# Seeding the banks of a down projection with the residual rows, in a decoder layer on one core

## The chip, the cores and the metric

The kernel is one program on 1 core of one Trainium2 chip. It computes one layer of a hybrid decoder on 256 rows of 2048 numbers, all in float32. The metric is device time in microseconds (us): the median of the runs.

The engines are named as in the profile: PE (TensorE, the products), PEld (its weight loads), DVE (VectorE), ACT (ScalarE), POOL (GpSimd) and SP, which issues most DMAs. A bank is one of the eight accumulators of 128 x 512 float32 in PSUM, into which PE writes its products and from which DVE and ACT read them.

## What is computed

The layer has three sub-layers, each followed by a LayerNorm over the sum of the scaled input and the sub-layer's result. The change is in the first and the third, two feed-forward networks (FFNs) of the same shape:

```python
D_MODEL, SEQ, D_FF = 2048, 256, 5632
DEEPNORM_ALPHA = (2.0 * DEPTH) ** 0.25        # DEPTH = 1
FFN_RES_WEIGHT = 0.5

def swiglu(x, w_gate, w_up, w_down):
    return (jax.nn.silu(x @ w_gate) * (x @ w_up)) @ w_down

x = layer_norm(DEEPNORM_ALPHA * x + FFN_RES_WEIGHT * swiglu(x, ffn1_w_gate, ffn1_w_up, ffn1_w_down), ln1_g, ln1_b)
# attention: two groups of heads, then layer_norm(DEEPNORM_ALPHA * x + mix, ln2_g, ln2_b)
x = layer_norm(DEEPNORM_ALPHA * x + FFN_RES_WEIGHT * swiglu(x, ffn2_w_gate, ffn2_w_up, ffn2_w_down), ln3_g, ln3_b)
```

A LayerNorm does not notice a common factor, so the kernel builds 2 * ALPHA * x + swiglu(x) and scales the epsilon by four.

## The kernel before

**Rows and products.** The 256 rows are two tiles t of 128. The residual stream lies in `y[t]`, 128 x 2048 in SBUF, in four column chunks n of 512. Every float32 product is made as three products of split numbers (`mm3`, lines 94 to 98): each operand is a high half (`whi` of a weight, `thi` of a row block) and a low half (`wlo`, `tlo`), and high x high (L96), high x low (L97) and low x high (L98) are added up in one bank. The halves are made by `split`: ACT casts the high half (L91), DVE subtracts it from the number to get the low half (L92).

**The blocks.** The work of an FFN is a list of steps (line 543): gate(0), up(0), gate(2), up(2), gate(4), down(0), up(4), gate(6), up(6), gate(8), down(1), up(8), then `last()` (the eleventh chunk of gate and up) and down(2). Gate and up make two chunks of 512 hidden columns each. After an up block the hidden columns are transposed by PE (`trans`, L463: four 128 x 128 transposes into one bank), copied out and split by ACT (L468, L470) and DVE (L471), while the next block runs. A down step takes the hidden columns of a group as the inner dimension and makes the four column chunks of the output: down(0) and down(1) have 8 pairs of inner blocks, down(2) has 6.

**One block (`gemm2`, line 251).** It makes a pair of column chunks j for both row tiles t, so four banks (t, j). The inner dimension comes in pairs i. A plain pair takes 8 `mm3`. A pair that is listed in `seven` takes 7, by Strassen's scheme: sums of the weights are made on DVE (L318 to L320) and sums of the rows (L390 to L393), and four of the products go to banks of their own, p1, p5, p6 and p7. Behind the last such pair these are read out once into four scratch tiles `rest` (L357 on ACT, L358 to L361 on DVE), while the plain pairs behind go on in the four banks (t, j). At the end of the block DVE adds each bank to its scratch tile (L370), and the block's `finish` is called with the result. So a block uses eight banks, and the pool has eight.

**What `finish` does.** For a gate block it is ACT's silu in place on the scratch tile (L479; in `last()` L510). For a down block it is `fin` (line 523), which adds the result to the rows: in down(0) `y = 2 * ALPHA * y + r` (L526), in down(1) and down(2) `y = r + y` (L528), each on DVE over 128 x 512. A down step calls `gemm2` twice, for the column pairs cp = 0 and 1; the second half of down(2) is made by `gemm` (line 540), chunk by chunk with 8 `mm3` a pair, and `fin` then reads the banks directly.

**What sets the order.** PE and SP keep the order in which the kernel's code issues their instructions. The instructions of ACT, DVE and POOL are put in an order by the scheduler, with its own costs, when the program is built; on the chip each engine works its queue off strictly in that order. A bank taken by `new_bank()` is free again when the last reader of its earlier tile is done. A block's pairs are in the order `DOWN` (4, 0, 1, 5, 2, 3, 6, 7), with 0 to 3 as the sevens; the first pair is plain, so it touches all four banks (t, j), in the order (0,0), (1,0), (0,1), (1,1), three products each.

Of the kernel before, what the change touches and what calls it, by code (L numbers as in the profile page):

```python
# [13 lines left out]
AF = mybir.ActivationFunctionType  # L14
OP = mybir.AluOpType
# [3 lines left out]
P = 128  # L19
D = 2048  # L20
S = 256
NT = S // P
FF = 5632
KD = D // P
NCH = 512
ALPHA = 2.0 ** 0.25
# [23 lines left out]
def layer(ctx: ExitStack, tc: tile.TileContext, a: dict, out: bass.AP):  # L50
    nc = tc.nc
    PE, V, A, G = nc.tensor, nc.vector, nc.scalar, nc.gpsimd
# [38 lines left out]
        A.copy(hi, src)  # L91
        V.tensor_tensor(lo, src, f(hi), op=OP.subtract)  # L92

    def mm3(ps, x, wh, wl, first, last):
        xh, xl = x
        PE.matmul(ps, xh, wh, start=first, stop=False)  # L96
        PE.matmul(ps, xh, wl, start=False, stop=False)  # L97
        PE.matmul(ps, xl, wh, start=False, stop=last)  # L98


    lanes, now, flags, held = {}, [0], {}, [False]
# [78 lines left out]
    def new_bank():  # L180
        return bank.tile([P, NCH], F32, name="bank")
# [66 lines left out]
                ahead[id(nxt[0]), nxt[1], nxt[2]] = load(nxt[0], nxt[1], [nxt[2] + j for j in range(KT)])  # L248
            finish(i, ps)

    def gemm2(x, xs, kps, seven, w, cp, finish, each=None, head=0, pre=None):

# [6 lines left out]
        B, todo = {}, []  # L261
# [10 lines left out]
        first, last = {}, {}  # L272
        for i, ops in todo:
            for o, op in enumerate(ops):
                first.setdefault(op[0], (i, o))
                last[op[0]] = (i, o)
        rest, heads = {}, []

        def weights(at, i):

# [45 lines left out]
        def mul(i, o, b, xp, name, wt):  # L326
            if b not in B:
                B[b] = new_bank()
            xp = sl(xs[i], xp) if isinstance(xp, int) else x(*xp)
            mm3(B[b], xp, *wt[name], first[b] == (i, o), last[b] == (i, o))  # L330

        for at, (i, ops) in enumerate(todo):
            if not s_at or at > s_at[-1]:
                held[0] = False
            wt = weights(at, i)
# [19 lines left out]
            if s_at and at == s_at[-1]:  # L355
# [6 lines left out]
                rest = {(0, 0): p1, (0, 1): q, (1, 0): u, (1, 1): z}  # L362
# [4 lines left out]
                each(at)  # L367
        for b in [(t, j) for t in range(NT) for j in range(2)]:
            if rest:
                V.tensor_tensor(rest[b], B[b], rest[b], op=OP.add)  # L370
            finish(*b, rest.get(b, B[b]))

    def new_T():
# [2 lines left out]
    def sl(pair, j):  # L376
        return pair[0][:, j, :], pair[1][:, j, :]


    ident = const.tile([P, P], F32, name="ident")  # L380
    make_identity(nc, ident)

    y = [const.tile([P, D], F32, name=f"y{t}") for t in range(NT)]
# [12 lines left out]
    def parts(s):  # L396
        hl = am2(F32R)
        split(*hl, s)
        return hl
# [48 lines left out]
    def ffn(name, x, xs, done, begin=None, after=None, late=()):  # L448
        wg, wu, wd = (W[name + n] + (W2[name + n][0],) for n in ("_w_gate", "_w_up", "_w_down"))
        groups = [[0, 1, 2, 3], [4, 5, 6, 7], [8, 9, 10]]  # L450
        late = list(late)
        hT, hS, hs, sg = {}, {}, {}, {}

        def trans(cs, ready, want=()):

            for c in cs:
                v, sums_too = [], c in want
                for t in range(NT):
                    while held[0] or now[0] < ready:
                        yield 1  # L460
                    pt = new_bank().rearrange("p (a b) -> p a b", a=4)
                    for j in range(4):
                        PE.transpose(pt[:, j, :], hs[c, t][:, j * P:(j + 1) * P], ident)  # L463
                    hT[c, t] = new_T()
                    src = pt
                    if sums_too:
                        src = wk([P, 4, P])
                        A.copy(src, pt)  # L468
                        v.append(src)
                    A.copy(hT[c, t][0], pt)  # L470
                    V.tensor_tensor(hT[c, t][1], src, f(hT[c, t][0]), op=OP.subtract)  # L471
                    if t and sums_too:
                        for i in range(KT):
                            hS[2 * c + i] = parts(sums([u[:, KT * i + j] for u in v for j in range(KT)]))
                    yield 1

        def gate(c0):
            def fin(t, j, r):
                A.activation(r, r, AF.Silu)  # L479
                sg[c0 + j, t] = r  # L480

            if c0:
                gemm2(x, xs, GATE, GATE7, name + "_w_gate", c0 // 2, fin)
                return
            def first(t, j, ps):
                sg[j, t] = wk([P, NCH])
                A.activation(sg[j, t], ps, AF.Silu)

            def rest(at):
                if begin and at == 7:  # L490
                    cst.update(load_consts())
                for _ in range(2):
                    if late:
                        late.pop(0)()

            gemm2(x, xs, GATE, (), name + "_w_gate", 0, first, each=rest, head=0 if begin else 4, pre=begin)

        def up(c0):
            def fin(t, j, r):
                hs[c0 + j, t] = sg[c0 + j, t]  # L500
                V.tensor_tensor(hs[c0 + j, t], r, sg[c0 + j, t], op=OP.mult)

            gemm2(x, xs, LATE if c0 in (4, 8) else UP, UP7, name + "_w_up", c0 // 2, fin, each=after if c0 == 0 else None)
            spawn(trans((c0, c0 + 1), now[0] + DFF, (0, 1, 4, 5, 9)), "T")

        def last():

            def fin(t, j, r):
                if j == 0:
                    A.activation(r, r, AF.Silu)  # L510
                    hs[10, t] = r
                else:
                    V.tensor_tensor(hs[10, t], r, hs[10, t], op=OP.mult)

            gemm2(x, xs, GATE, GATE7, name + "_gu", 0, fin)
            spawn(trans((10,), now[0] + DLAST), "T")

        def down(gi):
            grp = groups[gi]
            ks = list(range(grp[0] * 4, (grp[-1] + 1) * 4))  # L520
            xh = lambda k, t: sl(hT[k // 4, t], k % 4)

            def fin(t, n, ps):
                yc = y[t][:, n * NCH:(n + 1) * NCH]
                if gi == 0:
                    V.scalar_tensor_tensor(yc, yc, 2 * ALPHA, ps, op0=OP.mult, op1=OP.add)  # L526
                else:
                    V.tensor_tensor(yc, ps, yc, op=OP.add)  # L528
                if gi == 2:
                    done(t, n)  # L530

            for cp in range(2):
                if gi < 2 or cp == 0:
                    base = 2 * grp[0]
                    order, sevens = (DOWN, DOWN7) if gi < 2 else (range(6), (2, 3))
                    gemm2(xh, hS, [base + i for i in order], [base + i for i in sevens], name + "_w_down", cp,
                          lambda t, j, r: fin(t, 2 * cp + j, r))
                    continue
                for n in (2 * cp, 2 * cp + 1):
                    gemm(xh, wd, n, ks, lambda t, ps: fin(t, n, ps), tail=6 if n == 3 else 0)  # L540


        for step, n in ((gate, 0), (up, 0), (gate, 2), (up, 2), (gate, 4), (down, 0), (up, 4), (gate, 6), (up, 6), (gate, 8),
                        (down, 1), (up, 8)):
            step(n)
        last()
        down(2)
# [640 lines left out]
```

## Time and profile before

| | |
|---|---|
| median of 3 runs | 1764.81 us (1761.37 to 1767.2) |
| span of the profiled execution, first to last instruction | 1761.7 us |
| PE, PEld busy | 1741.7, 1429.6 us |
| DVE busy | 1596.9 us (2123 instructions) |
| ACT busy | 993.9 us (1306 instructions) |
| mean granted clock of TensorE | 0.998 |

The time of the profiled execution is known by its span; the median of the runs is 3.1 us above it. A row of the groups by line reads: line, engine, operation, result <- operands, shape, xcount | busy us, mean ns of one | idle time of the engine ahead of it, and what ended most of it. A row of a timeline reads: start in us from the span's start, how long, engine, line, operation, tiles, count, and in brackets the idle time ahead of it and what ended it; a row with x2 or x3 holds instructions that follow each other, with the time from the first's start to the last's end. A row of the list of waits reads: who <- whom, total us, times, longest us. A row of the windows reads: length, then for PE, PEld, DVE, ACT and POOL the busy us and the instructions, then PE's granted clock, the DMAs' share and their GB/s.

The first FFN runs from the start to about 697 us, the second from about 1060 us to the end. In the first, down(0) begins at 220, down(1) at 472 and down(2) at 638 us.

### The profile page before, as it was taken

Reading aid. Unit: us, or ns where it says so; the run is one execution under the profiler, and the core shown is the slowest. Engines: PE = TensorE matmul, PEld = TensorE weight load, DVE = VectorE, ACT = ScalarE, POOL = GpSimd, SP = SyncE. Lnnn points to the kernel's source line nnn. Section 1 sums busy time; section 2 is a strip of 40 time slices with the busy share of each in tenths; the row PEclk is TensorE's granted clock in tenths of the full one; section 3 lists DMA queues with packets and bytes.
Section 4 is the critical chain, followed back from the end, with each engine's and each line's share of the span. In section 5 each row is a group of like instructions: output and inputs, shape, how many; then the busy total and the mean of one; then the engine's idle time right before and its main releaser. Section 6 shows DMA issues by size and latency. Waiting matters only on the chain.

```text
span 1761.7 us, 22427 instructions
## 1 busy us (share of the span) xinstructions
PE 1741.7 (99%) x8058; PEld 1429.6 (81%) x8058; DVE 1596.9 (91%) x2123; ACT 993.9 (56%) x1306; POOL 17.0 (1%) x39
## 2 busy tenths in 40 slices
PE   9999999999999999999999999999999999999997
PEld 7888888888888888887788778888888878878886
DVE  7899999999999998765587679999999999999997
ACT  6656555574655565654455556565655565655651
POOL 0000000000000000000000000000000000000000
PEclk9999999999999999999999999999999999999999
DMA  9665666556656657545853355655566556556654
GB/s 334 218 211 178 204 204 203 191 184 212 197 196 225 204 172 255 181 139 206 283 195 111 132 168 179 203 179 203 192 206 222 201 181 215 191 193 217 203 200 159
DMA packets 103408, 350.01 MB, mean 199 GB/s; under 512 B 11136, under 2 KB 13696, under 8 KB 103296
## 3 DMA queue, kind: packets, MB, share of 16 engines
q1 hardware_dynamic: 102016, 344.39, 58.3%
q0 software_dynamic: 1280, 4.20, 0.9%
q8 instruction: 63, 1.03, 0.2%
q14 instruction: 49, 0.40, 0.1%
HBM read 346.44 MB, written 2.10 MB: 198 GB/s over the span
## 4 chain that ended last, share of the span: by engine, by line
PE 78%; DVE 14%; issue 3%; DMA 3%; ACT 2%; SPq 0%; DVEq 0%; POOL 0%; ACTq 0%; POOLq 0%
PE bank L97 24%; PE bank L96 24%; PE bank L98 24%; DVE wlo L92 6%; DVE sum L318 2%; DMA raw<-in_ffn_w_down 1%; DVE w L370 1%; ACT whi L91 1%; DVE sum L320 1%; DVE sum L319 1%; DMA raw<-in_ffn_w_up 1%; PE bank L1022 1%; DVE tlo L471 1%; PE bank L463 1%; PE bank L948 1%
## 5 line engine op out<-in xcount | busy, mean ns | idle before, releaser
L96 PE MATMUL bank<-whi,thi 128*128 128x512 f32 (+1 forms) x1934 | 761.6, 394 | 1.2 <-ACT whi L91 1.2
L97 PE MATMUL bank<-wlo,thi 128*128 128x512 f32 (+1 forms) x1934 | 751.6, 389 | 2.7 <-DVE wlo L92 2.5
L98 PE MATMUL bank<-whi,tlo 128*128 128x512 f32 (+1 forms) x1934 | 751.4, 389 | 0.0
L91 ACT CAST whi<-raw 128x1024 fp32r<-128x1024 f32 (+2 forms) x569 | 533.6, 965 | 272.1 <-PE bank L98 142.0
L92 DVE TENSOR_TENSOR wlo<-raw,whi 128x1024 fp32r<-128x1024 f32 (+2 forms) x569 | 624.8, 1113 | 53.5 <-ACT whi L91 52.6
L91 ACT CAST whi<-sum 128x1024 fp32r<-128x1024 f32 x267 | 278.9, 1050 | 366.4 <-DVE sum L320 140.1
L96 PEld LDWEIGHTS bank<-whi,thi 128*128 128x128 f32 x1934 | 363.2, 188 | 79.3 <-issue 4.1
L97 PEld LDWEIGHTS bank<-wlo,thi 128*128 128x128 f32 x1934 | 363.4, 188 | 75.9 <-DVE wlo L92 4.9
L98 PEld LDWEIGHTS bank<-whi,tlo 128*128 128x128 f32 x1934 | 363.0, 188 | 75.7
L92 DVE TENSOR_TENSOR wlo<-sum,whi 128x1024 fp32r<-128x1024 f32 x267 | 319.6, 1216 | 24.8 <-ACT whi L91 23.2
L97 PE MATMUL bank<-wlo,m 128*128 128x512 f32 x424 | 166.2, 392 | 2.4 <-DVE wlo L92 2.4
L98 PE MATMUL bank<-whi,m 128*128 128x512 f32 x424 | 165.1, 389 | 0.0
L96 PE MATMUL bank<-whi,m 128*128 128x512 f32 x424 | 165.0, 389 | 0.0
L318 DVE TENSOR_TENSOR sum<-raw 128x1024 f32<-128x1024 f32 x106 | 129.3, 1219 | 9.9 <-DMA raw<-in_ffn_w_down 5.4
L97 PEld LDWEIGHTS bank<-wlo,m 128*128 128x128 f32 x424 | 79.6, 188 | 22.6 <-DVE wlo L92 6.1
L96 PEld LDWEIGHTS bank<-whi,m 128*128 128x128 f32 x424 | 79.6, 188 | 16.8
L98 PEld LDWEIGHTS bank<-whi,m 128*128 128x128 f32 x424 | 79.6, 188 | 16.1
L370 DVE TENSOR_TENSOR w<-bank,w 128x512 f32<-128x512 f32 x120 | 79.0, 683 | 0.3
L320 DVE TENSOR_TENSOR sum<-sum,raw 128x512 f32<-128x512 f32 x106 | 72.6, 685 | 0.2
L319 DVE TENSOR_TENSOR sum<-sum,raw 128x512 f32<-128x512 f32 x106 | 72.6, 685 | 0.0
L773 ACT ACTIVATE w<-w,mx 128x256 f32<-128x256 f32 (+1 forms) x48 | 21.4, 446 | 30.4 <-DVE mx L769 27.4
L463 PEld LDWEIGHTS bank<-ident,w 128*128 128x128 f32 x176 | 21.9, 140 | 5.8
(188 smaller groups left out, 944.9 us busy)
## 6 DMA issues: line engine op xcount, KB each, us to landing
raw<-in_ffn_w_down SPq DMA_DIRECT2D x169, 512.0 KB, 4.8
raw<-in_ffn_w_up SPq DMA_DIRECT2D x160, 512.0 KB, 4.7
raw<-in_ffn_w_gate SPq DMA_DIRECT2D x146, 512.0 KB, 4.8
raw<-in_ffn_gu SPq DMA_DIRECT2D x32, 512.0 KB, 4.4
raw<-in_w_in SPq DMA_DIRECT2D x30, 512.0 KB, 4.8
raw<-in_w_out SPq DMA_DIRECT2D x20, 512.0 KB, 3.3
sum<-in_w_in SPq DMA_DIRECT2D x18, 512.0 KB, 5.9
sum<-in_ffn_w_gate SPq DMA_DIRECT2D x12, 512.0 KB, 4.4
```

Source lines behind the costliest of these rows:

```text
L91: A.copy(hi, src)
L92: V.tensor_tensor(lo, src, f(hi), op=OP.subtract)
L96: PE.matmul(ps, xh, wh, start=first, stop=False)
L97: PE.matmul(ps, xh, wl, start=False, stop=False)
L98: PE.matmul(ps, xl, wh, start=False, stop=last)
L318: V.tensor_tensor(t13, a_, b_[:, 1:2, :].broadcast_to([P, 2, NCH]), op=OP.add)
L319: V.tensor_tensor(t24[:, 0], t13[:, 0], a_[:, 1], op=OP.add)
L320: V.tensor_tensor(t24[:, 1], t24[:, 0], b_[:, 0], op=OP.add)
L370: V.tensor_tensor(rest[b], B[b], rest[b], op=OP.add)
L463: PE.transpose(pt[:, j, :], hs[c, t][:, j * P:(j + 1) * P], ident)
L471: V.tensor_tensor(hT[c, t][1], src, f(hT[c, t][0]), op=OP.subtract)
L773: A.activation(s[:, h, :], s[:, h, :], AF.Exp, bias=mx[:, h:h + 1], accum_out=sm[:, h:h + 1])
```

## The change

Ten blocks, the five calls of `gemm2` in the down steps of each FFN, get two new arguments. With `seed`, the four banks (t, j) are taken at the start of the block, and ACT writes the residual rows into them: an activation Identity of 128 x 512 from y, with the scale 2 * ALPHA in down(0) and 1 behind it. All products of the block are then added onto what is there (`onto`: none of them has the start flag). With `into`, the addition at the end of the block writes its result to y, and the separate operation that added it to y is gone. The second half of down(2) stays as it was. The four transposes of `trans` are written as products with the transpose flag, of which only the first into a bank has the start flag and only the last the stop flag.

```diff
-    def mm3(ps, x, wh, wl, first, last):
+    def mm3(ps, x, wh, wl, first, last, onto=False):
         xh, xl = x
-        PE.matmul(ps, xh, wh, start=first, stop=False)
-        PE.matmul(ps, xh, wl, start=False, stop=False)
-        PE.matmul(ps, xl, wh, start=False, stop=last)
+        PE.matmul(ps, xh, wh, start=first and not onto, stop=False, skip_group_check=onto)
+        PE.matmul(ps, xh, wl, start=False, stop=False, skip_group_check=onto)
+        PE.matmul(ps, xl, wh, start=False, stop=last, skip_group_check=onto)
...
         rest, heads = {}, []
+        if seed:
+            for b in [(t, j) for j in range(2) for t in range(NT)]:
+                B[b] = new_bank()
+                seed(*b, B[b])
...
-            mm3(B[b], xp, *wt[name], first[b] == (i, o), last[b] == (i, o))
+            mm3(B[b], xp, *wt[name], first[b] == (i, o), last[b] == (i, o), bool(seed) and not isinstance(b, str))
...
             if rest:
-                V.tensor_tensor(rest[b], B[b], rest[b], op=OP.add)
+                r = into(*b) if into else rest[b]
+                V.tensor_tensor(r, B[b], rest[b], op=OP.add)
+                rest[b] = r
             finish(*b, rest.get(b, B[b]))
...
-                        PE.transpose(pt[:, j, :], hs[c, t][:, j * P:(j + 1) * P], ident)
+                        PE.matmul(pt[:, j, :], hs[c, t][:, j * P:(j + 1) * P], ident, start=j == 0, stop=j == 3,
+                                  is_transpose=True, skip_group_check=True)
...
             def fin(t, n, ps):
-                yc = y[t][:, n * NCH:(n + 1) * NCH]
-                if gi == 0:
-                    V.scalar_tensor_tensor(yc, yc, 2 * ALPHA, ps, op0=OP.mult, op1=OP.add)
-                else:
-                    V.tensor_tensor(yc, ps, yc, op=OP.add)
-                if gi == 2:
-                    done(t, n)
+                V.tensor_tensor(rows(t, n), ps, rows(t, n), op=OP.add)
+                done(t, n)
...
                     gemm2(xh, hS, [base + i for i in order], [base + i for i in sevens], name + "_w_down", cp,
-                          lambda t, j, r: fin(t, 2 * cp + j, r))
+                          lambda t, j, r: done(t, 2 * cp + j) if gi == 2 else None, into=lambda t, j: rows(t, 2 * cp + j),
+                          seed=lambda t, j, b: A.activation(b, rows(t, 2 * cp + j), AF.Identity, scale=1.0 if gi else 2 * ALPHA))
                     continue
```

The new lines shift the line numbers: the seeds are L543, the silus L486 and L517 (before L479 and L510), the copies and casts behind transposes L475 and L477 (L468 and L470), the addition at the end of a block L375 (L370), the sums of weights L322 to L324 (L318 to L320).

On ACT, where gate(4) ends and down(0) begins in the first FFN: before, the casts behind the third and fourth transposes (`thi`), the four silus of gate(4) (`w`), and then the casts of weights.

```order
L470 CAST thi_2003<-bank_1998 128x512
L479 ACTIVATE w_1911<-w_1911 128x512
L479 ACTIVATE w_1912<-w_1912 128x512
L470 CAST thi_2024<-bank_2019 128x512
L479 ACTIVATE w_1913<-w_1913 128x512
L479 ACTIVATE w_1914<-w_1914 128x512
L91 CAST whi_2097<-sum_2081 128x1024
```

The same place of the changed kernel, where bank_2036, 2038, 2040 and 2042 are the four banks of down(0), in the order in which PE's products first reach them:

```order
L477 CAST thi_2003<-bank_1998 128x512
L486 ACTIVATE w_1911<-w_1911 128x512
L543 ACTIVATE bank_2036<-y0_92 128x512
L486 ACTIVATE w_1912<-w_1912 128x512
L477 CAST thi_2024<-bank_2019 128x512
L486 ACTIVATE w_1913<-w_1913 128x512
L486 ACTIVATE w_1914<-w_1914 128x512
L543 ACTIVATE bank_2038<-y1_93 128x512
L543 ACTIVATE bank_2040<-y0_92 128x512
L543 ACTIVATE bank_2042<-y1_93 128x512
L91 CAST whi_2101<-sum_2085 128x1024
```

The first seed stands behind the first silu, the other three behind the last. The order is the same where gate(8) ends and down(1) begins, and in the second FFN.

On ACT, where `last()` ends and down(2) begins in the first FFN, before: the cast of a weight, the copy (`w_5676`) and the cast of the last transposed block, the silu of the second row tile, and the casts of the row sums (`m`).

```order
L510 ACTIVATE w_5559<-w_5559 128x512
L91 CAST whi_5811<-raw_5799 128x512
L468 COPY w_5676<-bank_5669 128x512
L470 CAST thi_5674<-bank_5669 128x512
L510 ACTIVATE w_5561<-w_5561 128x512
L91 CAST m_5685<-w_5680 128x512
L91 CAST whi_5815<-sum_5802 128x1024
L91 CAST m_5693<-w_5688 128x512
```

The same place of the changed kernel; bank_5704 to 5710 are the four banks of down(2)'s first half:

```order
L543 ACTIVATE bank_5704<-y0_92 128x512
L543 ACTIVATE bank_5706<-y1_93 128x512
L475 COPY w_5676<-bank_5669 128x512
L477 CAST thi_5674<-bank_5669 128x512
L517 ACTIVATE w_5559<-w_5559 128x512
L517 ACTIVATE w_5561<-w_5561 128x512
L543 ACTIVATE bank_5708<-y0_92 128x512
L91 CAST m_5685<-w_5680 128x512
L91 CAST m_5693<-w_5688 128x512
L543 ACTIVATE bank_5710<-y1_93 128x512
L91 CAST whi_5815<-raw_5803 128x512
```

Two seeds stand ahead of the copy of the last transposed block, the third behind both silus, the fourth behind both casts of row sums.

On DVE, where the first half of down(0) ends and the second begins in the first FFN: before, the four additions at the end of the half (L370) and the four to y (L526), with the sums and low halves of the next half's weights around them.

```order
L319 TENSOR_TENSOR sum<-sum,raw 128x512
L92 TENSOR_TENSOR wlo<-raw,whi 128x512
L370 TENSOR_TENSOR w<-bank,w 128x512 x2
L526 SCALAR_TENSOR_TENSOR y_92<-y_92,w 128x512
L370 TENSOR_TENSOR w<-bank,w 128x512
L526 SCALAR_TENSOR_TENSOR y_93<-y_93,w 128x512
L526 SCALAR_TENSOR_TENSOR y_92<-y_92,w 128x512
L370 TENSOR_TENSOR w<-bank,w 128x512
L320 TENSOR_TENSOR sum<-sum,raw 128x512
L526 SCALAR_TENSOR_TENSOR y_93<-y_93,w 128x512
L92 TENSOR_TENSOR wlo<-sum,whi 128x1024 x2
```

In the changed kernel:

```order
L323 TENSOR_TENSOR sum<-sum,raw 128x512
L92 TENSOR_TENSOR wlo<-raw,whi 128x512
L324 TENSOR_TENSOR sum<-sum,raw 128x512
L375 TENSOR_TENSOR y_92<-bank,w 128x512
L375 TENSOR_TENSOR y_93<-bank,w 128x512
L375 TENSOR_TENSOR y_92<-bank,w 128x512
L375 TENSOR_TENSOR y_93<-bank,w 128x512
L92 TENSOR_TENSOR wlo<-sum,whi 128x1024 x2
```

The four operations on y are gone, and the last sum of the next half's weights stands ahead of the additions. PE's and SP's instructions stand in the same order as before.

More of the change, by code (lines that the diff above doesn't have):

```diff
@@ L249, in gemm_T, with gemm2 @@
             finish(i, ps)
-    def gemm2(x, xs, kps, seven, w, cp, finish, each=None, head=0, pre=None):
+    def gemm2(x, xs, kps, seven, w, cp, finish, each=None, head=0, pre=None, seed=None, into=None):
         src, pairs = W2[w]
@@ L521, in down, with rows @@
             xh = lambda k, t: sl(hT[k // 4, t], k % 4)
+            def rows(t, n):
+                return y[t][:, n * NCH:(n + 1) * NCH]
             def fin(t, n, ps):
-                yc = y[t][:, n * NCH:(n + 1) * NCH]
-                if gi == 0:
-                    V.scalar_tensor_tensor(yc, yc, 2 * ALPHA, ps, op0=OP.mult, op1=OP.add)
-                else:
-                    V.tensor_tensor(yc, ps, yc, op=OP.add)
-                if gi == 2:
-                    done(t, n)
+                V.tensor_tensor(rows(t, n), ps, rows(t, n), op=OP.add)
+                done(t, n)
             for cp in range(2):
```

## Prediction

> **What bounds the kernel now.** I read the page first, then the groups by line, then the list of waits, and last the timelines of PE, DVE and ACT where a gate block hands over to a down block.
>
> The page gives each engine's busy time, and the waits of PE come from the list of waits (total, times, longest).
>
> ```profile
> PE 1741.7 (99%) x8058; PEld 1429.6 (81%) x8058; DVE 1596.9 (91%) x2123; ACT 993.9 (56%) x1306; POOL 17.0 (1%) x39
> ...
> PE bank L97 <- DVE wlo L92: 4.8, 9, 0.9
> ```
>
> PE is idle for 20 us of the span of 1761.7. DVE at 91% looks like a second bound, yet in the whole kernel PE waits only 4.8 us for the low halves of weights that DVE makes (L92). The timeline of PE shows the longest such wait just behind a down block's change of column pair:
>
> ```profile
> 273.44 0.40 PE L96 MATMUL bank<-whi,m 128*128 128x512 f32 x1
> 274.34 0.50 PE L97 MATMUL bank<-wlo,m 128*128 128x512 f32 x1 [0.50 <-DVE wlo L92]
> 1573.58 0.50 PE L97 MATMUL bank<-wlo,m 128*128 128x512 f32 x1 [0.61 <-DVE wlo L92]
> ```
>
> The two idle times, 0.50 and 0.61, are all that relief of DVE at these places can give back, apart from drain around them: from 273.44 to 274.34 is 0.90 us, where these products otherwise start 0.23 us apart (three take 0.69, from 221.00 to 221.69 in the rows further down), so 0.67 is lost for 0.50 shown. So the kernel is bound by PE's own pace, and what PE is made to wait is added to the time.
>
> **What goes from DVE to ACT.** The groups by line show the operations that leave DVE and the nearest relatives of the one that ACT gets.
>
> ```profile
> L528 DVE TENSOR_TENSOR y<-w,y 128x512 f32<-128x512 f32 x24 | 16.0, 683 | 0.0
> L526 DVE SCALAR_TENSOR_TENSOR y<-y,w 128x512 f32<-128x512 f32 x16 | 10.6, 684 | 0.0
> L479 ACT ACTIVATE w<-w 128x512 f32<-128x512 f32 x32 | 19.4, 633 | 7.0 <-DVE w L370 7.0
> L357 ACT COPY w<-bank 128x512 f32<-128x512 f32 x30 | 17.3, 576 | 0.0
> L604 ACT ACTIVATE y<-y,mr,rstd 128x512 f32<-128x512 f32 x8 | 6.1, 812 | 1.0 <-DVE mr L599 0.9
> ```
>
> 24 + 16 = 40 operations leave DVE, 26.6 us of its busy time. The L370 additions stay and write y in place of scratch. ACT gets 40 activations of 128x512. No row shows ACT writing to a bank. The row nearest in form is L479 (activation, constant scale, same size): 0.63 us. The copy out of a bank (0.58) and the activation with two per-row operands (0.81) bound it. [...]
>
> The relief of DVE is worth what PE waited: 1.1 us idle by the two rows, times 0.67/0.50 for the drain, 1.5 us. It can't be above the 4.8 of the list, and not below nothing, since DVE loses work there and gains none.
>
> **What the change adds to PE.** The first product into each of the four banks of a seeded block now waits for its seed. A seed stands in ACT's queue at a fixed place, so it waits for all that stands ahead. Five blocks in each FFN are seeded; three of them follow a gate block (down(0), down(1), first half of down(2)), two follow another down half.
>
> *The two that follow a down half* cost nothing. Their banks held p1, p5, p6 and p7 of the half before, and the last of these is read by L361:
>
> ```profile
> 255.26 0.68 DVE L361 TENSOR_TENSOR w<-bank,w 128x512 f32<-128x512 f32 x1
> 257.84 0.63 ACT L91 CAST whi<-raw 128x512 fp32r<-128x512 f32 x1 [0.23 <-DMA raw<-in_ffn_w_down]
> 261.31 1.28 DVE L370 TENSOR_TENSOR w<-bank,w 128x512 f32<-128x512 f32 x2
> ```
>
> The last seed of the four stands ahead of the cast at 257.84, in time in which ACT waits for weights; PE ends the old half at about 261.3, when L370 reads its first bank. The cover is some 3 us; were it gone, each seed would cost up to 0.63.
>
> *down(0) and down(1)*, behind a gate block. These are the timelines of DVE, of ACT and of PE (which starts the three products of a bank about 0.23 apart) at the first such place.
>
> ```profile
> 219.18 0.68 DVE L370 TENSOR_TENSOR w<-bank,w 128x512 f32<-128x512 f32 x1
> 220.38 1.88 DVE L370 TENSOR_TENSOR w<-bank,w 128x512 f32<-128x512 f32 x3
> ...
> 219.90 0.63 ACT L479 ACTIVATE w<-w 128x512 f32<-128x512 f32 x1 [1.33 <-DVE w L370]
> 221.09 0.63 ACT L479 ACTIVATE w<-w 128x512 f32<-128x512 f32 x1 [0.56 <-DVE w L370]
> 221.63 0.57 ACT L470 CAST thi<-bank 128x512 fp32r<-128x512 f32 x1
> 222.10 1.15 ACT L479 ACTIVATE w<-w 128x512 f32<-128x512 f32 x2
> ...
> 219.86 0.60 PE L463 MATMUL bank<-ident,w 128*128 128x128 f32 x4
> 220.21 0.48 PE L96 MATMUL bank<-whi,thi 128*128 128x512 f32 x1
> 221.00 0.40 PE L96 MATMUL bank<-whi,thi 128*128 128x512 f32 x1
> 221.69 0.40 PE L96 MATMUL bank<-whi,thi 128*128 128x512 f32 x1
> ```
>
> PE begins the down block at 220.21 and its second bank at 221.00, while ACT is still at the silus of the gate block. Two activations in a row take 1.15, one 0.63, so the next starts 0.52 later. Seed 1 stands behind silu 1: it starts at 219.90 + 0.52 = 220.42 and lands at 221.05; with 0.04 for the hand-over (L370 ends at 219.86, the silu starts at 219.90) PE starts at 221.09 instead of 220.21, 0.9 late. Seed 2 stands behind silus 3 and 4: 222.10 + 2 x 0.52 = 223.14, landed 223.77, PE at 223.81 instead of 221.00: 2.8 late in all. Seeds 3 and 4 land at 224.29 and 224.81, PE wants them at 224.50 and 225.19: no more wait. So 2.8 us here.
>
> The rows of ACT's silus 3 and 4 and of PE's second bank at the other three places:
>
> ```profile
> 473.41 1.15 ACT L479 ACTIVATE w<-w 128x512 f32<-128x512 f32 x2
> 472.91 0.40 PE L96 MATMUL bank<-whi,thi 128*128 128x512 f32 x1
> 1268.73 1.15 ACT L479 ACTIVATE w<-w 128x512 f32<-128x512 f32 x2
> 1268.20 0.40 PE L96 MATMUL bank<-whi,thi 128*128 128x512 f32 x1
> 1520.33 1.15 ACT L479 ACTIVATE w<-w 128x512 f32<-128x512 f32 x2
> 1519.79 0.40 PE L96 MATMUL bank<-whi,thi 128*128 128x512 f32 x1
> ```
>
> Silu 3 plus 2 x 0.52 + 0.63 + 0.04 = 1.71, less PE's start: 2.2, 2.2 and 2.3. With the first, 9.5 us.
>
> *down(2), first half.* Seeds 1 and 2 now stand ahead of the copy of the last transpose. Seed 3 follows both silus, and seed 4 the two m casts, which wait for sums on DVE.
>
> ```profile
> 635.75 1.22 DVE L92 TENSOR_TENSOR wlo<-raw,whi 128x1024 fp32r<-128x1024 f32 x1
> 636.88 0.69 DVE L319 TENSOR_TENSOR sum<-sum,raw 128x512 f32<-128x512 f32 x1
> 640.48 0.28 DVE L390 TENSOR_TENSOR w<-w 128x128 f32<-128x128 f32 x1
> 642.50 0.28 DVE L393 TENSOR_TENSOR w<-w 128x128 f32<-128x128 f32 x1
> ...
> 636.41 0.59 ACT L470 CAST thi<-bank 128x512 fp32r<-128x512 f32 x1
> ...
> 638.33 0.48 PE L96 MATMUL bank<-whi,thi 128*128 128x512 f32 x1
> 640.50 0.39 PE L96 MATMUL bank<-whi,thi 128*128 128x512 f32 x1
> ```
>
> Seeds 1 and 2 start at about 636.9 and 637.4 and land before PE's 638.33 and the group behind it: no wait. For seed 4, DVE comes first. Behind L319 its order is now an L92 on a whole tile (1.13 to the next start, by 635.75 and 636.88), one split (L471), three L370 (0.60 apart, by the three in 1.88), and then the sums: 636.88 + 0.60 + 1.13 + 4 x 0.60 = 641.01. The sums take 2.30 (640.48 to 642.78), to 643.31; the m cast starts at 643.35, seed 4 0.52 later, lands at 644.50, and PE starts the fourth bank at 644.54 instead of 640.50: 4.0 late, seed 3's wait within it. The other FFN has the same orders: twice 4.0 is 8.0.
>
> What is queued behind the seeds on ACT is the cast of the sums' high halves, later by three starts of 0.52 at most, 1.6 us. PE comes to these weights 2.2 us and more later, so it is covered.
>
> The sum: 9.5 + 8.0 - 1.5 = **16.0 us**. The profiled span is 1761.7, so 1777.7; the runs' median, 1764.81, lies 3.1 above that span, and the forecast is 1764.8 + 16.0, rounded to **1781 us**.
>
> **Rivals.** *DVE is the bound and the seeds come in time* (not slower): the additions ahead of the silus would run earlier, because DVE has 26.6 us less to do, and the seeds with them; the gain is then at most PE's 4.8 us of waits, 1760.0 us. For it: DVE's 91%. It decides only if silu 4 is done about 2.2 to 2.8 us sooner, and against that stands that no operation leaves DVE ahead of the four additions in a gate block, and that even an idle DVE could add the last bank only after the product before the transposes at 219.86: 0.68 + 0.63 + 0.63 later is 221.80, still 0.8 past 221.00.
>
> *The clock falls in the waits.* If PE's clock halved for some us after each of the six, PE would lose about half of that time more. The windows show when it fell before (the seventh figure, behind the five engines, is the granted clock):
>
> ```profile
> 0.00:14.00 14.00, 10.97 (x32) 6.43 (x33) 7.69 (x18) 8.48 (x16) 1.75 (x13) 1.00 0.81 285
> 1756.00:1762.00 6.00, 0.00 (x0) 0.00 (x0) 2.74 (x5) 0.00 (x0) 0.00 (x0) 0.52 0.47 175
> ```
>
> 3 us of idle time spread over 14 left it at 1.00; it was down, at 0.52, only with PE out of work altogether. If it fell at each of the six places for as long as in that window, 6 us x 0.48 = 2.9 us each, 17 us would come on top: 1798 us. Against it stands that no single wait forecast here reaches 3 us. [...]
>
> *ACT's queue gives the delay on*: if the casts behind the seeds, 1.6 us late at six places, made PE wait again, 9.6 us more, 1790 us. PE's delay of 2.2 and more speaks against it.
>
> **How the numbers follow.** Forecast 0.79, DVE bound and seeds in time 0.09, clock 0.04, ACT's queue 0.08. Low end: waits of 0.8 at four places and half of 4.0 at two, less 1.5, is 5.7: 1770.5. High end: the third rival's 1790; seeds of 0.81 would add 0.4 at six places, 2.4, to the forecast alone, which stays inside. I take 1771 to 1790. About 0.3% (5.3 us) is what a measurement of this kernel can tell from no change. The first rival at its full gain (0.27%) lies within it, beyond it only if other waits go too: faster 0.03, same 0.07, slower 0.90.
>
> **What would show it.** PE should wait for ACT's seeds at L96 about 17 us in all, in some twelve waits, the longest of about 2 us, on the second bank of down(0) and down(1) and on the third and fourth of down(2); no such wait at the halves that follow a down half; the waits at 274.34 and 1573.58 gone; DVE's busy time down by about 27, ACT's up by about 25. If PE's waits for seeds sum to under 5 us, or a seed takes far from 0.63 us, the forecast is wrong.

## The result, and the profile after

The changed kernel took 1784.58 us in the median of 4 runs (1784.11 to 1786.5), the kernel before beside it 1764.34. The ratio is 1.0118, with a 95% interval of 1.0104 to 1.0132: slower by some 20 us. The profiled execution has a span of 1782.4 us against 1761.7, 20.7 more.

The page and the groups by line of the changed kernel: the first row is the busy time of the engines, the others are the seeds and the additions that now write y.

```profile
PE 1748.4 (98%) x8058; PEld 1433.5 (80%) x8058; DVE 1576.0 (88%) x2083; ACT 1019.0 (57%) x1346; POOL 17.0 (1%) x39
...
L543 ACT ACTIVATE bank<-y 128x512 f32<-128x512 f32 x40 | 22.9, 594 | 1.9 <-DVE w L365 1.1 <-DVE w L363 0.7
...
L375 DVE TENSOR_TENSOR y<-bank,w 128x512 f32<-128x512 f32 x40 | 25.1, 682 | 2.2 <-PE bank L98 2.2
```

The work moved as told: 40 instructions left DVE and 40 came to ACT, a seed takes 0.594 us, and ACT is 25.1 us busier. DVE is 20.9 us less busy and not 26.6. In a row of such additions one starts every 0.60 us although each lasts 0.68, which makes 40 x 0.60 = 24 of it; where the other 3 us are stays open.

What PE waits for, by the list of waits (total, times, longest):

```profile
PE bank L96 <- ACT bank L543: 12.0, 8, 3.0
PE bank L97 <- DVE wlo L92: 4.1, 7, 0.9
PE bank L96 <- DVE w L397: 3.0, 1, 3.0
```

The first row is new: PE waits for seeds. The third is one more of them, the third bank of down(2) in the second FFN, put down to the sum that the profile saw last. The second, which the relief of DVE was to shorten, stood at 4.8 before. By this list PE stood idle for seeds 15.0 us in all; with the drain around each wait it is 17.1, as added up below.

The timelines of ACT and of PE where down(0) of the first FFN begins:

```profile
219.12 0.63 ACT L486 ACTIVATE w<-w 128x512 f32<-128x512 f32 x1 [0.65 <-DVE w L375]
219.66 0.59 ACT L543 ACTIVATE bank<-y 128x512 f32<-128x512 f32 x1
220.32 0.63 ACT L486 ACTIVATE w<-w 128x512 f32<-128x512 f32 x1
220.86 0.57 ACT L477 CAST thi<-bank 128x512 fp32r<-128x512 f32 x1
221.32 1.15 ACT L486 ACTIVATE w<-w 128x512 f32<-128x512 f32 x2
222.37 1.63 ACT L543 ACTIVATE bank<-y 128x512 f32<-128x512 f32 x3
```

```profile
220.30 0.50 PE L96 MATMUL bank<-whi,thi 128*128 128x512 f32 x1
220.64 0.40 PE L97 MATMUL bank<-wlo,thi 128*128 128x512 f32 x1
220.87 0.40 PE L98 MATMUL bank<-whi,tlo 128*128 128x512 f32 x1
223.02 0.50 PE L96 MATMUL bank<-whi,thi 128*128 128x512 f32 x1 [1.75 <-ACT bank L543]
```

Seed 1 is in time. Seed 2 stands behind silus 2 to 4 and lands at about 222.96; PE, which wanted the second bank at 221.10, starts it at 223.02: 1.92 us lost. At the first product of down(2)'s third and fourth bank the same view of PE shows more than a wait:

```profile
643.09 0.39 PE L98 MATMUL bank<-whi,tlo 128*128 128x512 f32 x1
646.43 0.79 PE L96 MATMUL bank<-whi,thi 128*128 128x512 f32 x1 [2.95 <-ACT bank L543]
647.02 0.63 PE L97 MATMUL bank<-wlo,thi 128*128 128x512 f32 x1
647.45 0.63 PE L98 MATMUL bank<-whi,tlo 128*128 128x512 f32 x1
648.65 0.80 PE L96 MATMUL bank<-whi,thi 128*128 128x512 f32 x1 [0.57 <-ACT bank L543]
```

ACT's timeline has seed 3 right behind silu 2:

```profile
645.26 0.63 ACT L517 ACTIVATE w<-w 128x512 f32<-128x512 f32 x1 [0.56 <-DVE w L375]
645.80 0.58 ACT L543 ACTIVATE bank<-y 128x512 f32<-128x512 f32 x1
```

So PE has waits of 3.1 and 1.0 us, and from 646.43 on products of 0.63 us instead of 0.39, started 0.43 apart instead of 0.23. The windows over the wait and behind it name the cause (the seventh figure, behind the five engines, is PE's granted clock):

```profile
640.00:643.00 3.00, 3.00 (x17) 2.47 (x16) 3.00 (x4) 2.39 (x6) 0.00 (x0) 1.00 0.21 67
643.00:646.50 3.50, 0.55 (x4) 0.12 (x2) 3.50 (x9) 1.96 (x4) 0.00 (x0) 0.98 0.71 246
646.50:653.00 6.50, 5.93 (x13) 4.24 (x14) 6.50 (x14) 3.31 (x5) 0.00 (x0) 0.50 0.07 15
```

The clock was halved, at 0.50, in the 6.5 us behind the wait, and again at the same place of the second FFN (0.50 from 1704.50 to 1711.00). The loss of PE, in the table below too, is added up from the trace, over all products, as what a product starts later than the usual 0.23 us behind the one ahead of it: 17.1 us at ten waits for seeds, 5.6 us at products 0.43 apart, beyond those that the profile before has too. Together 22.7, for a span 20.7 us longer; the other stalls of PE came out 2.0 us shorter.

### The profile page after: what moved, and what is told of

The parts are those of the page before. It is cut to its first block, busy times and chain, and to the rows that moved or that the text cites. A ratio compares the mean times of both kernels' runs of the same rounds, so it can differ in the third digit from the quotient of the medians.

```text
span 1782.4 us, 22437 instructions
## 1 busy us (share of the span) xinstructions
PE 1748.4 (98%) x8058; PEld 1433.5 (80%) x8058; DVE 1576.0 (88%) x2083; ACT 1019.0 (57%) x1346; POOL 17.0 (1%) x39
## 3 DMA queue, kind: packets, MB, share of 16 engines
q8 instruction: 63, 1.03, 0.2%
## 5 line engine op out<-in xcount | busy, mean ns | idle before, releaser
L96 PE MATMUL bank<-whi,thi 128*128 128x512 f32 (+1 forms) x1934 | 765.0, 396 | 16.1 <-ACT bank L543 12.0
L322 DVE TENSOR_TENSOR sum<-raw 128x1024 f32<-128x1024 f32 x106 | 129.3, 1220 | 26.3 <-DMA raw<-in_ffn_w_up 22.7
L97 PEld LDWEIGHTS bank<-wlo,m 128*128 128x128 f32 x424 | 79.6, 188 | 20.7 <-DVE wlo L92 3.9
L324 DVE TENSOR_TENSOR sum<-sum,raw 128x512 f32<-128x512 f32 x106 | 72.7, 686 | 0.5
L375 DVE TENSOR_TENSOR w<-bank,w 128x512 f32<-128x512 f32 x80 | 52.0, 683 | 0.0
L778 ACT ACTIVATE w<-w,mx 128x256 f32<-128x256 f32 (+1 forms) x48 | 21.3, 446 | 30.3 <-DVE mx L774 27.4
L375 DVE TENSOR_TENSOR y<-bank,w 128x512 f32<-128x512 f32 x40 | 25.1, 682 | 2.2 <-PE bank L98 2.2
```

What stands on the lines that cost most here:

```text
L96: PE.matmul(ps, xh, wh, start=first and not onto, stop=False, skip_group_check=onto)
L97: PE.matmul(ps, xh, wl, start=False, stop=False, skip_group_check=onto)
L322: V.tensor_tensor(t13, a_, b_[:, 1:2, :].broadcast_to([P, 2, NCH]), op=OP.add)
L324: V.tensor_tensor(t24[:, 1], t24[:, 0], b_[:, 0], op=OP.add)
L375: V.tensor_tensor(r, B[b], rest[b], op=OP.add)
L778: A.activation(s[:, h, :], s[:, h, :], AF.Exp, bias=mx[:, h:h + 1], accum_out=sm[:, h:h + 1])
```

## The experiments

The theory was that the loss is the seeds' place in ACT's queue, and behind the long waits the halved clock. The rivals: that seeding itself costs, wherever it stands; that the changed flags of the transposes cost; that DVE's relief or a handed-on delay decides. Each row of the table is one kernel: the ratio to the kernel before measured beside it, and from its profiled execution the span above 1761.7, what of that PE lost at first products of seeded banks, at half-speed products, and the rest.

| kernel | median us | ratio (95%) | span | seeds | half speed | rest |
|---|---|---|---|---|---|---|
| no seeds, flags alone | 1764.77 | 0.9998 (0.9988 to 1.0007) | +3.1 | 0 | 0 | 3.1 |
| second halves alone | 1764.89 | 0.9998 (0.9989 to 1.0007) | +1.3 | 0 | 0 | 1.3 |
| down(0), down(1), seeds early | 1764.94 | 1.0007 (0.9996 to 1.0018) | +0.5 | 1.4 | 0 | -0.9 |
| all 40, seeds early | 1768.00 | 1.0017 (1.0007 to 1.0028) | +3.1 | 4.6 | 0 | -1.5 |
| down(2) alone | 1769.09 | 1.0031 (1.0021 to 1.0041) | +5.2 | 4.8 | 0 | 0.4 |
| down(0) and down(1) alone | 1778.24 | 1.0076 (1.0063 to 1.0089) | +14.3 | 9.7 | 4.3 | 0.3 |
| same, second seed one place later | 1780.84 | 1.0097 (1.0083 to 1.0110) | +16.9 | 12.6 | 7.3 | -3.0 |
| the change, first profile | 1784.58 | 1.0118 (1.0104 to 1.0132) | +20.7 | 17.1 | 5.6 | -2.0 |
| same, second seed two places later | 1786.46 | 1.0123 (1.0110 to 1.0137) | +26.1 | 16.1 | 7.1 | 2.9 |
| the change, once more | 1789.54 | 1.0145 (1.0129 to 1.0160) | +22.5 | 18.1 | 6.9 | -2.5 |
| first halves alone | 1792.60 | 1.0155 (1.0136 to 1.0173) | +32.4 | 21.3 | 12.1 | -1.0 |

The rest lies between -3.0 and +3.1 us: that is how much PE's other waits differ from one profiled execution to another. One part of it goes by the kernel, as the second experiment shows.

**No seeds.** Only the transposes' flags are changed; the residual rows are added on DVE as before.

```diff
+                    seeded = False
...
+                          into=(lambda t, j: rows(t, 2 * cp + j)) if seeded else None,
+                          seed=(lambda t, j, b: A.activation(b, rows(t, 2 * cp + j), AF.Identity,
+                                                             scale=1.0 if gi else 2 * ALPHA)) if seeded else None)
```

> No seeds at all: the adds of the residual rows are on VectorE as before, and what is left of the change is that the four transposes of a block go into their bank as one group, with one start flag. Theory: this costs nothing: 1764.3 us, within 2 us of it. Rival (the changed flags lengthen the transposes or delay the copies behind them): of 44 blocks of transposes, 0.3 us each, 1764.3 + 13 = 1777 us.

Measured: no difference (0.9998). The flags cost nothing; that rival is out.

**Seeds in the second halves alone.** The condition says which blocks are seeded; the others add on DVE.

```diff
+                    seeded = cp == 1
```

> Seeds in the second halves of down(0) and down(1) only (16 of the 40); every first half as before the change. Theory (TensorE is made to wait for seeds that stand behind silus and casts in ScalarE's queue, and only the first halves have those in front): no wait of TensorE for a seed over 0.1 us, VectorE about 11 us less busy than before, and the two waits of 0.50 and 0.61 us at 274.34 and 1573.58 may go, since they follow a second half: 1763.0 us, between 1761.5 and 1765. Rival (the seeding itself costs, 0.5 us of TensorE for each of the 40 wherever it stands): 1764.3 + 16 x 0.5 = 1772 us.

Measured: no difference (0.9998), no wait for a seed. Seeding as such costs nothing, and the cover argued for these halves is there. The timeline of PE still has the wait which the relief of DVE was to remove, 0.50 us at 274.34 before:

```profile
274.32 0.39 PE L96 MATMUL bank<-whi,m 128*128 128x512 f32 x1
275.32 0.50 PE L97 MATMUL bank<-wlo,m 128*128 128x512 f32 x1 [0.61 <-DVE wlo L92]
```

It had to be there. The expectation has this wait behind a second half, but it stands in the second half of down(0), which begins at about 261 us, behind the additions at the end of the *first* half. In this kernel these keep their separate operation on y (L535). The timeline of DVE at this place, and then the same place of the changed kernel:

```profile
264.69 1.28 DVE L535 SCALAR_TENSOR_TENSOR y<-y,w 128x512 f32<-128x512 f32 x2
267.10 0.68 DVE L535 SCALAR_TENSOR_TENSOR y<-y,w 128x512 f32<-128x512 f32 x1
267.70 2.35 DVE L92 TENSOR_TENSOR wlo<-sum,whi 128x1024 fp32r<-128x1024 f32 x2
...
262.06 2.48 DVE L375 TENSOR_TENSOR y<-bank,w 128x512 f32<-128x512 f32 x4
264.46 2.35 DVE L92 TENSOR_TENSOR wlo<-sum,whi 128x1024 fp32r<-128x1024 f32 x2
```

Without the operations on y, and with the last sum ahead of the additions, the low halves of the next sums come some 3 us sooner. The traces of all kernels agree on what that does to PE. In the four whose first halves of down(0) and down(1) are not seeded (before, flags alone, second halves alone, down(2) alone) PE loses 1.7, 3.6, 3.1 and 1.9 us to waits for DVE in the second halves of down(0) and down(1). In the eight profiled executions in which they are, no such wait there is longer than 0.15 us. So the relief of DVE does what was forecast, and it comes from the first halves.

**Seeds in the first halves alone.**

```diff
+                    seeded = cp == 0
```

> Seeds in the six first halves only (24 of the 40); the second halves of down(0) and down(1) as before the change. Theory: all of the loss is here, and the gain of 1.1 to 1.5 us behind the second halves is not: 1784.6 + 1.2 = 1786 us, between 1783.5 and 1788, with the same waits for seeds (12 us in 8 waits) and the same half-speed stretches after the two waits of 3.1 us in down(2). Rival (each seed costs 0.5 us): 1764.3 + 24 x 0.5 = 1776 us.

Measured: 1792.6 us. All of the loss is in the first halves, as the theory has it, but it is 7 us more than it expected. The timelines of ACT, of DVE and of PE at down(0) of the first FFN show why the first bank was late too, which it was not in the changed kernel's profile:

```profile
214.41 1.05 ACT L91 CAST whi<-raw 128x1024 fp32r<-128x1024 f32 x1 [2.01 <-DMA raw<-in_ffn_w_down]
215.37 0.58 ACT L477 CAST thi<-bank 128x512 fp32r<-128x512 f32 x1
221.90 0.63 ACT L486 ACTIVATE w<-w 128x512 f32<-128x512 f32 x1 [1.32 <-DVE w L375]
222.44 0.58 ACT L550 ACTIVATE bank<-y 128x512 f32<-128x512 f32 x1
...
215.98 0.69 DVE L478 TENSOR_TENSOR tlo<-bank,thi 128x512 fp32r<-128x512 f32 x1 [2.96 <-ACT thi L477]
...
223.07 0.50 PE L96 MATMUL bank<-whi,thi 128*128 128x512 f32 x1 [1.72 <-DVE w L375]
```

A load of weights came late: ACT's cast waited 2.0 us for it and started at 214.41, where it started at 211.63 in the changed kernel's profile and at 212.41 before. The cast of the transpose stood behind it, DVE waited 3.0 us for that, and so the additions, silu 1 and seed 1 came late. By the orders of before, as I read them, such a delay ends at the silus, whose results are needed only in the up block that follows. With the seed behind the silu it reaches PE. Two waits, of 1.88 and 1.93 us, stand 0.7 us apart here, and the half-speed products of this execution cost 12.1 us, at a mean granted clock of 0.990.

**The change once more**, unedited, to see whether it shows the same.

> The changed kernel itself once more, beside the others on this chip. If the extra 8 us of the kernel with seeds in the first halves alone are the times at which loads happened to land (in its profile the cast ahead of the first silu waited 2.0 us for a load, and so the first seed was late too), the changed kernel can show them too: anything from 1784 to 1795 us, and the profile says which by the waits on the first banks. If they come from the second halves that are not seeded there: 1784.6 us, within 2 us.

Measured: 1789.5 us, 1785.9 to 1792.1, and PE 1.03 us late at the first bank of down(0) against no wait there in the first profile. The cast that waits for the load started at 212.70 in this execution, against 211.63 in the first. So the time of the changed kernel itself varies, 1784.1 to 1792.1 over the two sets, with the waits on first banks (17.1 and 18.1 us in the two profiles) and the mean granted clock (0.994 to 0.991). Whether the remaining 3 us to the kernel with first halves alone are more than that stays open.

**Seeds early.** All 40, but each with priority.

```diff
-                seed(*b, B[b])
+                with tc.high_priority(): seed(*b, B[b])
```

> All 40 seeds, but each is given priority in the order of ScalarE's instructions: in down(0) and down(1) seeds 2 to 4 then stand right behind seed 1 and ahead of the silus 2 to 4, and in down(2) seeds 3 and 4 stand ahead of the silus. Theory (the place in ScalarE's queue is the cost): the waits of 1.9 us on the second bank and of 3.1 and 1.0 us in down(2) go, and with the 3.1 us the half-speed stretch behind them: 1784.6 - 15.9 - 6 = 1762.7 us, between 1760.5 and 1766, granted clock back at 0.998. Rival A (a bank comes free too late, so that the seed would wait wherever it stands): still over 1775 us. Rival B (VectorE bounds and the slower clock was chance): the time falls by the waits alone, 1784.6 - 15.9 = 1768.7 us.

Measured: 1768.0, 1.0017 of before: the loss of 20 to 25 us fell to about 3. That is 2 us above the range expected, and near the 1768.7 of rival B. But rival B has it that the time falls by the waits alone, and here the half-speed products went too. ACT's row at down(0) now holds all four seeds behind silu 1, and silus 2 to 4 (the second row) follow; below them is PE.

```profile
220.26 2.14 ACT L543 ACTIVATE bank<-y 128x512 f32<-128x512 f32 x4
...
222.82 1.67 ACT L486 ACTIVATE w<-w 128x512 f32<-128x512 f32 x3
...
220.90 0.50 PE L96 MATMUL bank<-whi,thi 128*128 128x512 f32 x1 [0.56 <-ACT bank L543]
221.70 0.40 PE L96 MATMUL bank<-whi,thi 128*128 128x512 f32 x1
...
645.47 0.66 PE L469 MATMUL bank<-ident,w 128*128 128x128 f32 x4 [0.69 <-DVE w L520]
```

The second bank starts without a wait, the granted clock is 0.998 as before, and no product ran at half speed. This is the experiment that settles the cause: the same seeds, the same work, the same order on PE, another place in ACT's queue. (Some operations of ACT and DVE on weights and row sums changed places with them.) Two costs stay: waits of 0.5 to 1.2 us on first banks and on a bank of down(2) that comes free late (4.6 us), and a transpose in down(2) that waits for a product of gate and up (L520; 0.85 us in each FFN). The seeds delay the silus ahead of L520, but these were done at 643.08, and DVE came to L520 at 644.73, behind seven operations of the row sums; before, the first such product (L513) stood ahead of them all, at 639.88. So this wait is one of DVE's order, and not of a delay that ACT's queue gives on.

**Seeds early in down(0) and down(1), none in down(2).** The silus of the gate block are issued behind the seeds as well.

```diff
-                seed(*b, B[b])
+                with tc.high_priority(): seed(*b, B[b])
+            while silus:
+                A.activation(silus[0], silus[0], AF.Silu)
+                silus.pop(0)
...
-                A.activation(r, r, AF.Silu)
+                if c0 in (4, 8):
+                    silus.append(r)
+                else:
+                    A.activation(r, r, AF.Silu)
...
+                    seeded = gi < 2
```

> down(0) and down(1) seeded (32 of the 40 seeds; down(2) adds its rows on VectorE as before), the seeds with priority and the silus of the gate block ahead of them issued behind the four seeds, so that all four stand ahead of the first silu, which waits for VectorE. Theory (the whole cost is the place in ScalarE's queue and the clock that follows idle time): no wait for a seed over 0.2 us in the first halves, no half-speed products, granted clock 0.998, and 32 adds less on VectorE. If VectorE's relief is worth the 1.1 to 1.5 us that were forecast: 1763.4 us, and faster than the kernel before by up to 0.1%; if it is worth nothing: 1764.8 us, no difference. Rival (delayed silus are handed on to the transposes and to TensorE): 1766 us or more, with waits of TensorE at the transposes of the next blocks.

Measured: 1764.94, 1.0007 (0.9996 to 1.0018), no difference. The four seeds came right behind silu 1, not ahead of it, and 1.4 us of waits on first banks remain. PE's waits for DVE in the second halves, 1.7 us before, are gone with the 32 additions, but besides the 1.4 us some 1.0 us came in at two transposes in down(2), which wait for a product of gate and up as above, though down(2) has no seeds here. The sum is 0.7 us, the span 0.5 longer. So the gain of DVE's relief is there and is used up, and the kernel is not faster than before.

**Seeds in down(2) alone.**

```diff
+                    seeded = gi == 2
```

> Seeds in the first half of down(2) alone (8 of the 40), as the changed kernel has them; down(0) and down(1) as before. Theory: of the changed kernel's loss only this part stays, 4.0 us of waits and 2.5 to 3.4 us of half-speed products in each FFN: 1764.8 + 2 x (4.0 + 2.8) = 1778 us, between 1775 and 1781. Waits alone, without the clock: 1773 us.

Measured: 1769.1, a miss by 9 us. With down(0) and down(1) unseeded the order came out otherwise, as the timeline of ACT shows; below it is PE's third bank.

```profile
638.08 1.10 ACT L550 ACTIVATE bank<-y 128x512 f32<-128x512 f32 x2
640.07 0.64 ACT L517 ACTIVATE w<-w 128x512 f32<-128x512 f32 x1
640.60 1.12 ACT L550 ACTIVATE bank<-y 128x512 f32<-128x512 f32 x2
...
641.25 0.50 PE L96 MATMUL bank<-whi,thi 128*128 128x512 f32 x1 [0.88 <-ACT bank L550]
```

Seed 4 now stands right behind seed 3 and ahead of the m casts, and PE loses 4.8 us in both FFNs instead of 8.2, with no half-speed product (granted clock 0.998). So it speaks for the place in the queue once more, but not for a fixed price of a seed in down(2), on which the expectation rested.

**Seeds in down(0) and down(1) alone.**

```diff
+                    seeded = gi < 2
```

> Seeds in down(0) and down(1) only (32 of the 40); down(2) adds its rows on VectorE as before. Theory (waits for late seeds, and in down(2) alone a wait long enough to halve TensorE's clock): the waits on the second banks stay, 1.92 + 0.14 + 1.93 in the first FFN and 1.92 + 1.01 + 1.93 in the second, 8.9 us, and no product runs at 0.427 us: 1764.7 + 8.9 = 1773.6 us, between 1771 and 1776, granted clock 0.998. So down(2) is worth 1784.6 - 1773.6 = 11 us, of which 8.2 us are its waits and the rest the clock. Rival (the clock falls anyhow, the wait ahead of it is chance): half-speed products somewhere, and 1776 to 1779 us.

Measured: 1778.2, 13.4 us above before, which is the rival's range and not the theory's. The waits are about as expected (9.7 for 8.9), but half-speed products cost 4.3 us, at a mean granted clock of 0.995, and so the clean run that was expected did not come. Two of its places have the same wait; the windows over each wait and behind it:

```profile
478.50:481.70 3.20, 1.44 (x6) 1.05 (x6) 3.20 (x5) 3.20 (x7) 0.00 (x0) 1.00 0.01 4
481.75:485.17 3.42, 3.42 (x10) 2.64 (x9) 3.39 (x5) 1.70 (x2) 0.00 (x0) 0.50 0.49 153
...
1533.10:1536.40 3.30, 1.55 (x7) 0.98 (x6) 3.30 (x6) 3.30 (x8) 0.00 (x0) 1.00 0.13 48
1536.50:1539.90 3.40, 3.40 (x17) 2.81 (x16) 3.40 (x5) 1.93 (x2) 0.00 (x0) 1.00 0.46 154
```

Behind a wait of 1.92 us the clock was 0.50 for 3.4 us in one place and 1.00 in the other. The length of the wait does not separate the two.

**The second seed one place, and two places, later**, to lengthen the same waits without added work.

```diff
-                seed(*b, B[b])
+            for b in [(0, 0), (0, 1), (1, 0), (1, 1)] if cp == 0 else list(B):
+                seed(*b, B[b])
```

(Two places later: `[(0, 0), (0, 1), (1, 1), (1, 0)]`.)

> As the run before (down(0) and down(1) seeded, down(2) not), but in the first halves the seed of the second bank that TensorE needs is written third instead of second, so that TensorE waits one seed longer at four places, about 1.93 + 0.54 = 2.5 us; no work is added. Waits alone: 1773.6 + 4 x 0.54 = 1775.8 us. If the clock falls after an idle time of 2.5 us: 2.8 us more at each place, 1787 us. If it takes about 3 us of idle time close together, then only in down(1) of the second FFN, where a wait of 1.0 us stands 0.7 us ahead: 1778.6 us.

> As the run before, but the seed of the second bank is written last of the four, so that TensorE waits two seeds longer, about 1.93 + 1.07 = 3.0 us at four places. Waits alone: 1773.6 + 4 x 1.07 = 1777.9 us. If about 3 us of idle time halve TensorE's clock for some 6 us, as in down(2) of the changed kernel: 4 x 2.8 us more, 1789 us, with products 0.427 us apart behind each of the four waits.

Measured: 1780.8 and 1786.5. The waits grew as told, to 2.44 and 2.96 us. Of the first kernel's four places three fell to half speed, at a mean granted clock of 0.994; the second's half-speed products cost no more in all, 7.1 us against 7.3, at the same 0.994. The forecasts of a fall at every place (1787 and 1789) and of none (1775.8 and 1777.9) both missed the first; the second lies nearer to a fall at every place. The rows of the first kernel's places are in the last section; the length of the wait doesn't separate them.

No kernel here beats the one before; the nearest are equal to it.

## Why the prediction was right, and where it was not

**The bound.** That PE's own pace bounds, and that what PE is made to wait is added to the time, held in every run: in the table the losses of PE account for the span within 3.1 us.

**The gain of DVE**, forecast at 1.5 us, is there in the traces. The two waits that it was read from are gone in the changed kernel's profile, and PE's loss in the second halves of down(0) and down(1) is 1.7 to 3.6 us in the four executions without the relief and none with it. No run shows it as a shorter time: where the seeds cost least, other waits used it up.

**The halves behind another down half** cost nothing, as forecast: no wait for a seed, ratio 0.9998.

**down(0) and down(1)**, forecast 9.5 us in four places: 1.92, 0.14 + 1.93, 1.92 and 1.01 + 1.93 in the profile, 8.9 in all. The mechanism, seed 2 behind silus 3 and 4, is the one in the rows. At the first place silu 1 ran at 219.12, 0.9 us sooner against PE than in the profile before (219.90), and the wait is 0.9 shorter than forecast. That was luck of one execution: the load ahead of it landed sooner (cast at 211.63, before at 212.41). In the change once more, with the cast at 212.70, the place cost 1.03 + 1.92, close to the 2.8 forecast. The prediction took the times of one profile as fixed, and the first banks hang on when loads land. A seed took 0.59 us for 0.63.

**down(2)**, forecast 4.0 us each: 3.11 + 0.97 and 3.18 + 0.97, 8.2 for 8.0. The sum gave no split: it took seed 4 as the late one, with seed 3's wait within it. In the run seed 3 brought most of it. Silu 2 waited for DVE to 645.26, so seed 3 came at 645.80, and its wait alone was 3.1.

**The clock, the rival given 0.04, came true in part.** The step that failed is "no single wait forecast reaches 3 us", taken as a reason against it; that 3 us are needed was the author's estimate. Two did, and in the kernel with down(0) and down(1) alone a wait of 1.92 us had a clock of 0.50 behind it. The prediction's own 4.0 us at down(2) stood in two waits close together, and the row of 0 to 14 us that it set against the rival was no evidence: half of its 3 us lie ahead of the first product, at 1.52, and behind that no single wait up to 14 us is longer than 0.76 us (the one that ends at 13.25). The halved clock cost 5.6 us in this profile, 2.8 at each of two places, close to the rival's 2.9; the rival had it at all six. Term by term the span rose by waits of 17.1 (forecast 17.5), less 2.0 at other stalls (forecast 1.5), and by the clock's 5.6, for which the sum had nothing: 20.7 for 16.0.

**DVE as the bound** (forecast 0.09) is out: the seeds came late, and the relief of DVE took away those waits in the second halves and no more. **The handed-on delay** (0.08) doesn't show in the changed kernel; where seeds were put ahead of the silus a transpose lost 0.85 us in each FFN, by DVE's order.

**The signs named** were there: waits for seeds of 17.1 us for the 17 forecast (15.0 in the list of waits), in ten places rather than twelve, the longest 3.2 rather than 2, on the banks named; ACT's busy time rose by 25.1 (forecast 25), DVE's fell by 20.9 (forecast 27).

## What to carry to other kernels

An operation moved to an engine with idle time cost what stood ahead of it in that engine's queue, not its own duration: the same 40 seeds cost 20 to 25 us behind the silus and about 3 ahead of most of them. Look in the order of the receiving engine, and at which of its waits (here a load, and DVE's additions) then reach the engine that bounds. And before a relief is called worthless, look which operations stand ahead of the wait that it is to remove: the waits of half a microsecond were gone in every execution that took away the additions ahead of them, and in none that took away others. Such a gain, some 2 us here, is soon lost again to waits that the moved work brings.

## What the runs showed of the hardware

TensorE's clock halved behind shorter waits than expected: 1.92 us, with 0.50 over the 3.42 us behind it, in the kernel with down(0) and down(1) alone, where no half-speed product was expected. Rows of PE in the kernel with the second seed one place later, at the ends of its three half-speed stretches:

```profile
229.46 0.63 PE L97 MATMUL bank<-wlo,thi 128*128 128x512 f32 x1
229.89 0.44 PE L98 MATMUL bank<-whi,tlo 128*128 128x512 f32 x1
230.16 0.40 PE L96 MATMUL bank<-whi,thi 128*128 128x512 f32 x1
...
1284.57 0.45 PE L97 MATMUL bank<-wlo,thi 128*128 128x512 f32 x1
1284.86 0.40 PE L98 MATMUL bank<-whi,tlo 128*128 128x512 f32 x1
...
1540.50 0.48 PE L97 MATMUL bank<-wlo,thi 128*128 128x512 f32 x1
1540.82 0.39 PE L98 MATMUL bank<-whi,tlo 128*128 128x512 f32 x1
```

A product at full speed starts 0.23 us behind the last, one at half speed 0.43. The starts 0.43 apart end at 229.89, 1284.57 and 1540.50, and from 230.16, 1284.86 and 1540.82 on they are 0.23 apart again. The windows behind the waits of 2.4 us at down(0) and at down(1) of the first FFN in this kernel:

```profile
223.70:229.80 6.10, 6.05 (x14) 4.81 (x15) 4.49 (x5) 2.53 (x3) 0.00 (x0) 0.50 0.26 89
...
481.00:487.00 6.00, 6.00 (x28) 4.95 (x27) 5.68 (x7) 2.68 (x4) 0.00 (x0) 1.00 0.35 99
```

The timeline of PE has 2.27 us of idle time at both, and the wait on the first bank ahead of them is 0.44 us at the one and 0.51 at the other. Behind the first the clock was 0.50 for 6.1 us, behind the second 1.00. So the length of the wait separates the places neither at 2.4 nor at 1.92 us, and what does is not shown. In the changed kernel the waits of 3.1 and 1.0 us in down(2) had a clock of 0.50 for 6.5 us behind them in both FFNs, and the wait of 1.92 us at down(0) of the first FFN one of 1.00 (223.15 to 226.56). All this was found from the traces afterwards; no run was made to test it ahead.
